# RWKV recurrence with 120 instructions of scheduler priority in a hybrid trunk layer

## The chip, the cores and the metric

The kernel runs on one core of one Trainium2 chip. The metric is the device time of one execution in microseconds (us); of several runs the median is shown. The engines are TensorE (PE in the rows, with PEld for its weight loads), VectorE (DVE), ScalarE (ACT), GpSimd (POOL) and SyncE (SP), which issues most of the DMA. Each engine has a queue of its own and works through it in order.

## The reference

One layer of a trunk with three token mixers side by side, for 512 tokens of width 1024, in float32:

```python
h = rms_norm(x)
u, q, k, v, r_k_v_and_low_rank, gates = split(h @ w_in)
y0 = s5(u)                       # complex diagonal SSM, 32 groups x 16 channels, 64 states, then GLU
y1 = diff_attention(q, k, v)     # 4 heads, two softmaxes each
y2 = rwkv7(r, w, k, v, a, b)     # 8 heads of 64, one state matrix per head
x = x + (sum_i sigmoid(gate_i) * (y_i @ w_branch_i)) @ w_out
x = x + swiglu(rms_norm(x))
```

What the change touches is the third mixer. Its state is a 64x64 matrix per head that every token updates:

```python
sa = state @ a_t
state = state * w_t + outer(sa, b_t) + outer(v_t, k_t)
y_t = state @ r_t
```

## The kernel before

**Layout.** Activations are held transposed: the 1024 channels lie on 8 tiles of 128 partitions, the 512 tokens are the free dimension. A float32 operand is split into a high and a low part, and a product is three matmuls: high times high (L1301), low times high (L1302), high times low (L1303); the attention's value projection has the same three with the operands swapped (L1285 to L1287). Each 128x512 block of weights is loaded into the ring `wr`, cast to its high part `wh` on ACT (L1229), and its low part `wl` is subtracted out on DVE (L1230). These dense projections are the bulk of TensorE's work and run through the whole kernel.

**The recurrence.** The 8 heads of RWKV are taken in 4 pairs, two heads side by side on 128 partitions, and the 512 tokens in 8 chunks of 64. What a chunk needs of itself is prepared in parallel for all chunks (`local`, `inverse`, `join`). What is left is serial: `chain(p)` of `Rwkv`, L599 to L655, walks through the 8 chunks of a pair and hands the state Z from one to the next. One step is a ring of eight links on three engines:

- PE L623: the state meets the chunk; DVE L625, twice (one per head): the result leaves PSUM and `uv` is added to it. In the first chunk there is no state yet, and two copies on DVE (L619, L620) stand in their place;
- PE L630: the inverse of the chunk is applied; ACT L631: its copy out of PSUM;
- PE L635: the update of the state; DVE L650, twice: the new state Z, for the next L623;
- off the ring: PE L638 and L640 (the output y), ACT L642 (its copies), ACT L654 (the state times its decay).

Between these links the queues hold work of other parts: dense matmuls, the S5 mixer (`cmul`, L710 to L715 on DVE, and L943 to L947 on POOL, and the matmuls L1005 and L1009), attention (L1087 to L1199), the casts of weights.

**After the recurrence** `finish(p)` normalizes the pair's output: an inverse square root on eight numbers per partition (`rsqrt`, a shift and three Newton steps of L243, L244 and L246 on DVE), its copy to 512 columns (DVE L267), its transposition to all heads (PE L269, four of 128 columns), and DVE L671, L673 and L676, which take it out of PSUM and apply it.

**What sets the order.** The Python text issues the parts as a string says, where a letter is a part and its digits the pair or quarter (C is `chain`, F `finish`, Q a quarter of S5, X, K and A attention, G gates, I and J the inverse and the join):

```python
ORDER = ("L R00 G1 R01 R02 P0 T0 I0 R10 R12 S R11 U0 P1 R20 R22 R21 T1 H0 G1 J0 U1 I1 J1 C0 P2 T2 F0 U3 U2 Q0 C1 G3 Q1 G2 H1 I2 Q2 R31 "
         "F1 R32 R30 P3 T3 J2 G1 I3 J3 C3 G1 Q3 X0 K0 A0 G2 Y0 C2 Y1 Y2 Y3 F3 X1 K1 G1 A1 F2 X2 K2 O0 O2 O3 G2 A2 X3 K3 G3 O1 A3")
```

A scheduler of the framework then simulates the engines and puts the instructions into their queues. An instruction's priority is its place in the program; of those that are ready in its simulation, the one with the smallest goes first. So the parts are interleaved, and a part issued later fills what an earlier one leaves free. PSUM has eight banks: two for the dense products, three for RWKV, three for the rest.

In the trace pair 0 runs its chain from 157 to 191 us, pair 1 from 218 to 257, pair 3 from 346 to 373, and pair 2 from 373 to 408.

Of the kernel before, what the change touches and what calls it, by code (L numbers as in the profile page):

```python
# [34 lines left out]
NSPLIT = (6, 3, 2, 3)  # L35
ORDER = ("L R00 G1 R01 R02 P0 T0 I0 R10 R12 S R11 U0 P1 R20 R22 R21 T1 H0 G1 J0 U1 I1 J1 C0 P2 T2 F0 U3 U2 Q0 C1 G3 Q1 G2 H1 I2 Q2 R31 "
         "F1 R32 R30 P3 T3 J2 G1 I3 J3 C3 G1 Q3 X0 K0 A0 G2 Y0 C2 Y1 Y2 Y3 F3 X1 K1 G1 A1 F2 X2 K2 O0 O2 O3 G2 A2 X3 K3 G3 O1 A3")
DECAY_C = 0.5 * math.exp(-0.5)

PCOLS = {}  # L40
# [232 lines left out]
class Rwkv:  # L273
# [90 lines left out]
    def _prep(self, p):  # L364
# [20 lines left out]
        cum3 = cum.rearrange("p (c t) -> p c t", t=CH)  # L385
        nc.scalar.activation(W[:, :, 1:CH + 1], cum3, AF.Exp, scale=-DECAY_C)
        wc = E.small("wc", [P, NCH], bufs=5)
        nc.gpsimd.tensor_copy(wc, W[:, :, CH])
        IW = E.slot("IW")
        nc.scalar.activation(IW, cum, AF.Exp, scale=DECAY_C)  # L390
        E.free(cum)
# [1161 lines left out]
def trunk_kernel(ctx: ExitStack, tc: tile.TileContext, A, outT):  # L1553
# [46 lines left out]
    rw = Rwkv(E, (A["w_lora"], A["g2"]))  # L1600
# [31 lines left out]
    prs, qs, qkv = [None] * 4, [None] * 4, [None] * 4  # L1632
# [4 lines left out]
            E.free(rw.xw, rw.xa)  # L1637

    def chain(p):
        rw.chain(prs[p])  # L1640

    def finish(p):
        rw.finish(p, prs[p], ydr[2][p])
# [19 lines left out]
    def glu(i):  # L1663
        gh, gl = br[0]
        dense(A["w_glu"][i], 4, lambda k: gh[:, k], lambda k: gl[:, k], lambda ps: s5.finish(i, ps, ydr[0][i]))

    step = dict(T=lambda p: rw.local(prs[p]), L=lora, R=rw_in, P=prep, I=lambda p: rw.inverse(prs[p]), J=lambda p: rw.join(prs[p]), C=chain, S=s5.params, H=s5.phases, U=s5_in, Q=s5.quarter,
                F=finish, X=att_q, K=att_kv, A=att, G=gate, Y=gelu, O=glu)
    for t in ORDER.split():
# [179 lines left out]
```

## Time and profile before

| | |
|---|---|
| three runs, us | 1003.09, 1004.07, 1008.0 (median 1004.07) |
| the profiled execution | 1011.66 us, of which its span is 1009.9 us |
| granted clock of TensorE, mean | 0.988 |
| PE busy | 970.1 us (96% of the span) |
| PEld busy | 824.2 us (82%) |
| DVE busy | 754.3 us (75%) |
| ACT busy | 473.5 us (47%) |
| POOL busy | 143.3 us (14%) |
| the chain of work that ended last | PE 77%, DVE 15%, DMA 3% |

A row of the timeline has the start and the length in us, the engine, the line of the kernel, the operation, what it writes and reads, the shapes, and in brackets the idle time of its engine ahead of it and what ended that. A row of the windows has a stretch, its length, each engine's busy time and number of instructions, the granted clock of TensorE (1.00 is 2.4 GHz, 0.50 is 1.2 GHz), the busy share of the DMA engines and GB/s.

### The profile page before, as it was taken

The numbers are of one execution on the slowest core, as the hardware profiler recorded it, in microseconds if no ns is written. First come the engines' busy times: TensorE is split into PE (matmuls) and PEld (weight loads), VectorE is DVE, ScalarE is ACT, GpSimd is POOL, SyncE is SP. The second block draws the span as 40 slices with busy tenths as digits, with TensorE's granted clock in tenths as the row PEclk, the third lists the DMA queues.
The fourth block names the chain that finished last, engine by engine and source line by source line (L and its number), as shares of the span: only waits on it lengthen the run. The fifth ranks groups of instructions, "written<-read, shape, count | busy, mean of one in ns | idle before, by whom it ended". The sixth has DMA issues, their size and how long they took to land.

```text
span 1009.9 us, 17883 instructions
## 1 busy us (share of the span) xinstructions
PE 970.1 (96%) x6416; PEld 824.2 (82%) x6416; DVE 754.3 (75%) x1941; ACT 473.5 (47%) x978; POOL 143.3 (14%) x176
## 2 busy tenths in 40 slices
PE   7989999899999999999999999989999999999998
PEld 5777777676779777888887788879999999988886
DVE  6899676789994789977867655679989998943331
ACT  6534333434342566446446324566666666632220
POOL 2021120422420001000000332011211221000000
PEclk9999899999998999999999999999999999999999
DMA  7325242221431334252448864476776677354440
GB/s 241 116 53 133 64 110 78 84 56 53 100 96 40 95 105 116 84 156 75 154 149 270 273 194 159 138 178 165 151 163 175 152 153 170 79 155 123 131 136 27
DMA packets 105593, 129.95 MB, mean 129 GB/s; under 512 B 45376, under 2 KB 47296, under 8 KB 105504
## 3 DMA queue, kind: packets, MB, share of 16 engines
q1 hardware_dynamic: 99168, 117.28, 38.7%
q0 software_dynamic: 6336, 11.54, 7.4%
q8 instruction: 50, 0.82, 0.3%
q14 instruction: 39, 0.32, 0.1%
HBM read 109.90 MB, written 18.88 MB: 128 GB/s over the span
## 4 chain that ended last, share of the span: by engine, by line
PE 77%; DVE 15%; DMA 3%; ACT 2%; issue 2%; POOL 1%; SPq 0%; DVEq 0%; ACTq 0%; POOLq 0%
PE bank L1391 21%; PE bank L1302 13%; PE bank L1303 13%; PE bank L1301 13%; DVE wl L1230 2%; DMA ar<-in_w_ffn_in 1%; DMA ar<-ymix 1%; PE bank L468 1%; PE bank L479 1%; PE bank L1188 1%; PE bank L262 1%; PE bank L630 1%; PE bank L1285 1%; PE bank L1286 1%; PE bank L1287 1%
## 5 line engine op out<-in xcount | busy, mean ns | idle before, releaser
L1229 ACT CAST wh<-wr 128x512 fp32r<-128x512 f32 x198 | 120.4, 611 | 208.8 <-PE bank L1302 163.6
L1230 DVE TENSOR_TENSOR wl<-wr,wh 128x512 fp32r<-128x512 f32 x198 | 136.8, 693 | 82.8 <-ACT wh L1229 82.3
L1301 PE MATMUL bank<-act_hi,wh 128*128 128x512 f32 x360 | 150.5, 418 | 7.8 <-ACT wh L1229 5.9
L1302 PE MATMUL bank<-act_lo,wh 128*128 128x512 f32 x360 | 149.7, 416 | 0.8 <-DVE act_lo L257 0.7
L1303 PE MATMUL bank<-act_hi,wl 128*128 128x512 f32 x360 | 149.6, 416 | 0.0
L1391 PE MATMUL bank<-sp_t,wh 128*128 128x256 f32 x528 | 97.5, 285 | 1.1 <-ACT ar L1423 0.8
L1391 PE MATMUL bank<-act_hi,wh 128*128 128x256 f32 x352 | 98.0, 278 | 0.0
L1391 PE MATMUL bank<-act_hi,wl 128*128 128x256 f32 x352 | 97.7, 278 | 0.1
L1391 PE MATMUL bank<-act_lo,wh 128*128 128x256 f32 x352 | 97.5, 277 | 0.0
L1301 PEld LDWEIGHTS bank<-act_hi,wh 128*128 128x128 f32 x360 | 70.0, 195 | 22.7 <-ACT wh L1229 5.9
L1391 PEld LDWEIGHTS bank<-sp_t,wh 128*128 128x128 f32 x528 | 82.7, 193 | 1.5 <-ACT ar L1423 1.0
L1302 PEld LDWEIGHTS bank<-act_lo,wh 128*128 128x128 f32 x360 | 70.0, 194 | 16.4 <-DVE act_lo L257 3.5
L1303 PEld LDWEIGHTS bank<-act_hi,wl 128*128 128x128 f32 x360 | 70.0, 194 | 14.4 <-issue 0.6
L1391 PE MATMUL bank<-sp_t,wl 128*128 128x256 f32 x264 | 75.2, 285 | 0.0
L1301 PE MATMUL bank<-act,wh 128*128 128x512 f32 x176 | 68.5, 389 | 0.0
L1302 PE MATMUL bank<-act,wh 128*128 128x512 f32 x176 | 68.5, 389 | 0.0
L1303 PE MATMUL bank<-act,wl 128*128 128x512 f32 x176 | 68.5, 389 | 0.0
L1391 PEld LDWEIGHTS bank<-act_hi,wl 128*128 128x128 f32 x352 | 66.2, 188 | 0.7 <-DVE wl L254 0.7
L1391 PEld LDWEIGHTS bank<-act_hi,wh 128*128 128x128 f32 x352 | 66.4, 189 | 0.3
L1391 PEld LDWEIGHTS bank<-act_lo,wh 128*128 128x128 f32 x352 | 66.4, 189 | 0.0
L253 ACT CAST wh<-ar 128x512 fp32r<-128x512 f32 x79 | 48.2, 622 | 28.1 <-DMA ar<-in_w_ffn_in 18.1
L254 DVE TENSOR_TENSOR wl<-ar,wh 128x512 fp32r<-128x512 f32 x79 | 53.1, 685 | 9.4 <-ACT wh L253 8.9
(491 smaller groups left out, 2217.7 us busy)
## 6 DMA issues: line engine op xcount, KB each, us to landing
wr<-in_w_in SPq DMA_DIRECT2D x88, 256.0 KB, 2.9
ar<-in_w_ffn_in SPq DMA_DIRECT2D x46, 256.0 KB, 3.2
wr<-in_w_ffn_out SPq DMA_DIRECT2D x40, 256.0 KB, 2.7
gate<-ar SPq DMA_DIRECT2D x24, 256.0 KB, 2.4
wr<-in_w_branch SPq DMA_DIRECT2D x24, 256.0 KB, 3.6
ar<-gate SPq DMA_DIRECT2D x24, 256.0 KB, 3.6
ar<-in_w_ffn_in POOLq DMA_DIRECT2D x22, 256.0 KB, 3.9
sp_raw<-in_w_ffn_in SPq DMA_DIRECT2D x21, 256.0 KB, 3.4
```

Of the source, the lines that this page charges most:

```text
L253: nc.scalar.copy(hi, src)
L254: nc.vector.tensor_tensor(lo, src, hi.bitcast(F32), ALU.subtract)
L262: self.nc.tensor.matmul(ps[:, b, :], sq[:, b * P:(b + 1) * P], self.c("sel"), start=True, stop=True)
L468: nc.tensor.matmul(pa[:, c * P:(c + 1) * P], kb[rows, 4 * q + c].rearrange("p a t -> p (a t)"), ar[rows, 4 * q + c].rearrange("p a t -> p ...
L479: nc.tensor.matmul(pt[64:128, w], aam[q][0:64, c, h, 1], uv[0:64, 4 * q + c, h * CH:(h + 1) * CH], start=True, stop=True)
L630: nc.tensor.matmul(pu[:, 0:P], yt[:, c0:c0 + 2].rearrange("p c t -> p (c t)"), ts, start=True, stop=True)
L1229: nc.scalar.copy(wh, raw)
L1230: nc.vector.tensor_tensor(wl, raw, wh.bitcast(F32), ALU.subtract)
L1301: nc.tensor.matmul(ps, wh[:, j], hi(k), start=k == 0, stop=False)
L1302: nc.tensor.matmul(ps, wh[:, j], lo(k), start=False, stop=False)
L1303: nc.tensor.matmul(ps, wl[:, j], hi(k), start=False, stop=k == nk - 1)
L1391: nc.tensor.matmul(ps, w[x][:, c], b(y, j), start=first and j == js[0] and n == 0, stop=last and j == js[-1] and n == 2, skip_group_check= ...
```

## The change

Everything that `chain` issues gets a priority 120 places ahead of its own. The computation, the tiles and the set of instructions on every engine stay as they are; only the order of the queues differs. Lines after the new constant are one higher, those after `chain(p)` three higher.

```diff
+CHAIN_AHEAD = 120
 DECAY_C = 0.5 * math.exp(-0.5)
...
     def chain(p):
-        rw.chain(prs[p])
+
+        with tc.high_priority(offset=CHAIN_AHEAD):
+            rw.chain(prs[p])
```

The queues of PE, DVE and ACT differ from about 155 us of the trace on and are the same again after about 445 us. In that stretch the chain's matmuls stand 5 places earlier on PE on average (from 7 later to 16 earlier), its DVE instructions 3 and its ACT instructions one. On POOL and on SP a few instructions change places with a neighbour.

The first place is on DVE, in the seventh chunk of pair 0. L619 and L620 are already the first copies of pair 1's chain; `s_rr`, `s_ri` and the `ar` tiles of L710 to L714 are S5's. Before:

```order
L650 SCALAR_TENSOR_TENSOR rw_Z_220<-bank_86,wc_rw_472,Zw_rw_1487 64x64 x2
L711 TENSOR_TENSOR ar_14_82<-s_ri_806,ar_14_82 128x512
L625 TENSOR_TENSOR rw_T_223<-bank_85,ar_2_70 64x64 x2
L712 TENSOR_TENSOR ar_12_80<-ar_12_80,ar_14_82 128x512
L619 COPY rw_T_223<-ar_5_73 64x64
L620 COPY rw_T_223<-ar_5_73 64x64
L714 TENSOR_TENSOR ar_14_82<-s_ri_806,ar_14_82 128x512
L650 SCALAR_TENSOR_TENSOR rw_Z_221<-bank_87,wc_rw_472,Zw_rw_1501 64x64 x2
```

And now (a line number is one higher, so L651 is L650 of before):

```order
L651 SCALAR_TENSOR_TENSOR rw_Z_220<-bank_86,wc_rw_472,Zw_rw_1487 64x64 x2
L711 TENSOR_TENSOR ar_12_80<-s_rr_805,ar_14_82 128x512
L626 TENSOR_TENSOR rw_T_223<-bank_85,ar_2_70 64x64 x2
L712 TENSOR_TENSOR ar_14_82<-s_ri_806,ar_14_82 128x512
L620 COPY rw_T_223<-ar_5_73 64x64
L621 COPY rw_T_223<-ar_5_73 64x64
L713 TENSOR_TENSOR ar_12_80<-ar_12_80,ar_14_82 128x512
L651 SCALAR_TENSOR_TENSOR rw_Z_221<-bank_87,wc_rw_472,Zw_rw_1501 64x64 x2
L715 TENSOR_TENSOR ar_14_82<-s_ri_806,ar_14_82 128x512
```

The chain's instructions have moved up by one S5 product each: L714 of before now stands behind the second L650, and four other instructions still stand between L625 and L650.

The second place is on DVE, at the end of `finish(0)` and the first chunk of pair 1. `rqt_rw`, `rqy_rw` and `ri_rw` are the Newton steps of that `finish`, the small `ar` tiles those of S5. Before:

```order
L710 TENSOR_TENSOR ar_6_74<-s_rr_805,ar_14_82 128x512
L246 SCALAR_TENSOR_TENSOR ri_rw_480<-rqt_rw_487,rqy_rw_494 128x8
L711 TENSOR_TENSOR ar_13_81<-ar_12_80 128x8x2
L713 TENSOR_TENSOR ar_12_80<-ar_12_80 128x8x2
L267 COPY ar_8_76<-ri_rw_480 128x512
L712 TENSOR_TENSOR ar_12_80<-ar_12_80,ar_13_81 128x8x2
L714 TENSOR_TENSOR ar_13_81<-ar_12_80 128x8x2
L711 TENSOR_TENSOR ar_12_80<-s_ri_806,ar_14_82 128x512
L715 TENSOR_TENSOR ar_12_80<-ar_12_80,ar_13_81 128x8x2
L710 TENSOR_TENSOR ar_12_80<-ar_12_80 128x8x4
L671 TENSOR_TENSOR ar_7_75<-ar_7_75,bank_86 128x512
```

And now, from the same S5 product on:

```order
L711 TENSOR_TENSOR ar_6_74<-s_rr_805,ar_14_82 128x512
L244 TENSOR_TENSOR rqt_rw_487<-rqy_rw_494 128x8
L712 TENSOR_TENSOR ar_13_81<-ar_12_80 128x8x2
L714 TENSOR_TENSOR ar_12_80<-ar_12_80 128x8x2
L245 TENSOR_TENSOR rqt_rw_487<-rqt_rw_487,rqx_rw_481 128x8
L713 TENSOR_TENSOR ar_12_80<-ar_12_80,ar_13_81 128x8x2
L715 TENSOR_TENSOR ar_13_81<-ar_12_80 128x8x2
L247 SCALAR_TENSOR_TENSOR ri_rw_480<-rqt_rw_487,rqy_rw_494 128x8
L711 TENSOR_TENSOR ar_12_80<-ar_12_80 128x8x4
L716 TENSOR_TENSOR ar_12_80<-ar_12_80,ar_13_81 128x8x2
L268 COPY ar_8_76<-ri_rw_480 128x512
```

L267 (now L268) has moved behind four small instructions of S5 that stood behind it: L712, L714, L710 and L715. The last L243 and L244 of the Newton steps have moved behind the S5 product L710 that opens both pieces. Behind L268 nine small instructions follow, and then L672 (L671 of before). On PE one dense matmul that stood ahead of the four L269 now stands behind them; between them and L635 there are five, as before.

The third place is on DVE at about 410 us, where `finish(2)` and attention run. `wl_116` is the low part of a weight block of the value projection. Before:

```order
L243 TENSOR_TENSOR rqt_rw_487<-rqi_rw_483 128x8
L244 TENSOR_TENSOR rqt_rw_487<-rqt_rw_487,rqx_rw_481 128x8
L1230 TENSOR_TENSOR wl_116<-wr_114,wh_115 128x512
L246 SCALAR_TENSOR_TENSOR rqy_rw_490<-rqt_rw_487,rqi_rw_483 128x8
L243 TENSOR_TENSOR rqt_rw_487<-rqy_rw_490 128x8
```

And now:

```order
L1164 TENSOR_REDUCE mx_s_3362<-bank_89 128x1
L677 SCALAR_TENSOR_TENSOR ar_7_75<-ar_8_76,pcol,bank_86 128x512
L1163 TENSOR_TENSOR bank_90<-bank_90,const 128x128
L247 SCALAR_TENSOR_TENSOR rqy_rw_972<-rqt_rw_969,rqi_rw_965 128x8
L1097 TENSOR_TENSOR ar_11_79<-bank_83,ar_11_79 64x512
L1164 TENSOR_REDUCE mx_s_3362<-bank_90 128x1
L244 TENSOR_TENSOR rqt_rw_969<-rqy_rw_972 128x8
L1231 TENSOR_TENSOR wl_116<-wr_114,wh_115 128x512
L1169 TENSOR_TENSOR nb_s_3371<-mx_s_3362,nrq_s_3759 128x2
```

The low part of that block now stands behind 30 instructions more, down to L1096 (now L1097), while the first matmul that reads it (L1287) stands where it stood, but for one place.

## Rows read from the trace of the kernel before

**Rows 1.** The page's span, and busy time of each engine.
```profile
span 1009.9 us, 17883 instructions
...
PE 970.1 (96%) x6416; PEld 824.2 (82%) x6416; DVE 754.3 (75%) x1941; ACT 473.5 (47%) x978; POOL 143.3 (14%) x176
```

**Rows 2.** Windows of 50 us in the stretch that the change reorders.
```profile
200.00:250.00 50.00, 46.33 (x352) 35.72 (x351) 45.40 (x129) 18.49 (x45) 13.83 (x18) 1.00 0.21 56
...
400.00:450.00 50.00, 48.60 (x294) 40.30 (x293) 42.90 (x139) 26.03 (x61) 1.27 (x1) 1.00 0.39 119
```

**Rows 3.** Waits of PE: us in total, times, the longest.
```profile
PE bank L623 <- DVE rw_Z L650: 5.4, 3, 3.3
PE bank L269 <- DVE ar L267: 3.1, 3, 1.4
...
PE bank L635 <- DVE ar L671: 1.8, 1, 1.8
...
PE bank L630 <- DVE rw_T L625: 0.8, 3, 0.4
...
PE bank L1183 <- DVE ar L1179: 0.6, 1, 0.6
```

**Rows 4.** Timeline of DVE from 179.4 to 186.4 us, seventh chunk of pair 0.
```profile
179.47 0.89 DVE L711 TENSOR_TENSOR ar<-s_ri,ar 128x512 f32<-128x512 f32 x1
...
180.89 0.98 DVE L712 TENSOR_TENSOR ar<-ar,ar 128x512 f32<-128x512 f32 x1
181.90 1.16 DVE L619 COPY rw_T<-ar 64x64 f32<-64x64 f32 x1
183.09 1.14 DVE L620 COPY rw_T<-ar 64x64 f32<-64x64 f32 x1
184.26 1.52 DVE L714 TENSOR_TENSOR ar<-s_ri,ar 128x512 f32<-128x512 f32 x1
185.82 0.58 DVE L650 SCALAR_TENSOR_TENSOR rw_Z<-bank,wc_rw,Zw_rw 64x64 f32<-64x64 f32 x2
```

**Rows 5.** Timeline of POOL in the same stretch.
```profile
181.40 1.61 POOL L945 TENSOR_TENSOR ar<-ar 128x512 f32<-128x512 f32 x1
183.09 1.10 POOL L947 TENSOR_TENSOR ar<-s_pi,ar 128x512 f32<-128x512 f32 x1
```

**Rows 6.** Windows: behind the wait at 186 us, and around `finish(0)`.
```profile
187.00:190.40 3.40, 3.40 (x13) 2.84 (x11) 2.75 (x7) 1.58 (x3) 1.12 (x2) 0.50 0.42 109
...
222.50:229.10 6.60, 3.35 (x17) 2.21 (x16) 6.60 (x12) 1.21 (x2) 6.44 (x5) 1.00 0.30 84
```

**Rows 7.** Timeline of DVE from 223.9 to 228.2 us, `finish(0)` among S5.
```profile
223.96 1.07 DVE L713 TENSOR_TENSOR ar<-ar 128x16 f32<-128x16 f32 x1
224.95 0.41 DVE L267 COPY ar<-ri_rw 128x512 f32<-128x512 f32 x1
225.29 1.25 DVE L712 TENSOR_TENSOR ar<-ar,ar 128x16 f32<-128x16 f32 x1
226.46 0.17 DVE L714 TENSOR_TENSOR ar<-ar 128x16 f32<-128x16 f32 x1
...
227.15 1.07 DVE L715 TENSOR_TENSOR ar<-ar,ar 128x16 f32<-128x16 f32 x1
```

**Rows 8.** Timeline of POOL, first and last of five S5 products there.
```profile
222.29 1.63 POOL L943 TENSOR_TENSOR ar<-s_pr,ar 128x512 f32<-128x512 f32 x1 [11.31 <-DMA gate<-ar]
...
228.15 1.14 POOL L946 TENSOR_TENSOR ar<-s_pr,ar 128x512 f32<-128x512 f32 x1
```

**Rows 9.** Timeline of PE, dense matmuls behind L635, five apart.
```profile
229.59 0.40 PE L1301 MATMUL bank<-act_hi,wh 128*128 128x512 f32 x1
...
230.76 0.39 PE L1303 MATMUL bank<-act_hi,wl 128*128 128x512 f32 x1
```

**Rows 10.** Window from the end of L1230 for `wl_116` to the end of L1096.
```profile
410.45:419.46 9.01, 8.95 (x59) 7.81 (x59) 8.71 (x29) 5.01 (x10) 0.00 (x0) 1.00 0.17 58
```

**Rows 11.** Timeline of PE: the first matmul that reads `wl_116`.
```profile
417.31 0.28 PE L1287 MATMUL bank<-wl,act_hi 128*128 128x256 f32 x1
```

## The prediction

> **What bounds the kernel now.** I read the page's shares first: PE is busy 970.1 of 1009.9 us [rows 1]. So the kernel is a full TensorE queue with some 40 us of holes, and a new order can win only holes, or make new ones. The reader should next see how far the other engine of the chain has room: DVE is busy 45.40 of 50 us in the window from 200 us and 42.90 in the one from 400 us [rows 2]. An instruction that is moved up in such a queue puts something else back, and what is put back may be wanted too.
>
> Then the waits of PE [rows 3]. Three kinds belong to the recurrence: L623 for the new state (5.4 us in three waits, one of them 3.3), L630 for its operand (0.8), and L635 for a PSUM bank that L671 of `finish` holds (1.8). That is 8.0 us, all that the change aims at, 0.8% of the span. The same view shows that `finish` is as much in the way: L269 waits for L267 three times, 3.1 us in all.
>
> The timeline of the longest wait tells what it is made of [rows 4]. After L625 the DVE queue holds L712, L619, L620 and L714 (0.98 + 1.16 + 1.14 + 1.52 = 4.80 us), and only then L650, for which PE waits. Beside it stands POOL's timeline [rows 5]: L945 ends at 181.40 + 1.61 = 183.01 and the copy L619 at 181.90 + 1.16 = 183.06; L947 ends at 184.19 and the copy L620 at 184.23. Two 64x64 copies of over 1.1 us, each ending 0.04 to 0.05 us after a POOL product: DVE stands still until POOL is done. The Trainium skill gives the reason ("SBUF — State Buffer", section "Who interferes with whom"): the two engines share a pair of ports, the one that holds it keeps it for its whole instruction, and the other blocks. By that rule, with which the trace agrees, an instruction that is moved up one place only meets the next POOL product; were the ports shared by the cycle, term 1 would be at its lower end.
>
> **The change part by part.** No instruction is added or removed, so every term is a wait that shrinks, grows or is new. The profiled execution took 1011.66 us (span 1009.9), 7.6 us or 0.76% above the median of the three runs, 1004.07; the sum is made against the profiled one and its difference is applied to the median. A measurement of this kernel can tell about 0.5%, 5 us, from no change.
>
> *Term 1, the wait of 3.3 us (first place in the order).* L714 moves behind L650, but another S5 product, L711, comes from ahead of L625 to behind it, and the copies of pair 1's chain, which have the same priority, stay in between. Four instructions as before. If each kept the length of its row [rows 4], the queue would shrink by 1.52 - 0.89 = 0.63 us, which is the most. If each waits for a POOL product as the copies do, their number is the same and only an earlier start is left. PE itself arrives earlier too, since one matmul fewer stands between L623 and L630. I take -0.2 us, near the reading that the copies' rows show, between -0.6 and +0.5 (two matmuls of cover lost).
>
> *Term 2, `finish(0)` (second place).* Its L267 moves behind L712, L714, L710 and L715. The first and the last took 1.25 and 1.07 us [rows 7], beside five POOL products that run from 222.29 to 229.29 [rows 8]; L714 took 0.17, and L710 is of its size. That is 2.7 us. L269 starts 2.7 us later, and as one dense matmul (0.23 us, from five steps in 230.76 - 229.59 = 1.17 [rows 9]) now stands behind it, its wait grows by 2.9, from 1.4 to 4.3. Behind L267 the queue to L671 becomes shorter: those four are gone from there (2.7), and nine small ones come (1.5 at 0.17). A 512-wide product leaves as well; I set it against the later of the nine being wider. With the same five matmuls of cover on PE the wait of L635 shrinks by 1.2, from 1.8 to 0.6. Together +2.9 - 1.2 = +1.7 us. Below: the four meet no POOL product and cost 0.17 each, 0.7 in all; 0.7 + 0.2 - 1.2 = -0.3. Above: three more POOL products at 1.1 are waited for, and L635 gains nothing: +3.5. I take +1.7, since the rows show every S5 product there held that reads two tiles while POOL works.
>
> *Term 3, the weight block at 410 us (third place).* The low part `wl_116` is ready at 410.45, where the window [rows 10] begins, 6.9 us before its first use at 417.31 [rows 11]. That distance is its cover. It now stands behind everything down to L1096: 29 instructions, with 8.71 us of DVE in 9.01 [rows 10], so DVE has no slack there to catch up. It is ready at 410.45 + 8.71 = 419.16, and PE waits 1.85 us. The wait of L1183 for L1179 (0.6) [rows 3] comes 5 us later, is DVE's too, and is then covered. +1.2 us, between 0 (pair 2's chain has released DVE two microseconds sooner) and +2.5 (nothing is given back, and the few small ones that come in addition count).
>
> *The rest of the chains.* Pair 2 has the most other work between its links: on PE 137 other instructions before and 127 now, on DVE 76 and 70. Ten matmuls of 128 to 512 columns are 1.2 to 2.3 us of cover that PE no longer has when it reaches a link; six DVE instructions at 42.90/139 = 0.31 [rows 2] are 1.9 us of queue that the link no longer stands behind. They cancel. Pairs 1 and 3 lose three or four matmuls each. I take 0, between -1.5 and +1.5. POOL and SP swap neighbours only; no transfer is among PE's waits in this stretch, so that costs nothing, and if one came late it would show as a wait of L1301 for L1229.
>
> The sum is -0.2 + 1.7 + 1.2 + 0 = **+2.7 us**: 1014.4 for a profile like this one, and 1004.07 + 2.7 = **1006.8 us** for the median. With the terms' lower ends it would be -2.4 (1001.7); upper ends together lead into the second rival.
>
> **The rivals.** *The waits of the chain go.* If DVE serves each link at once, 8.0 us go. Behind the longest wait PE also ran at half its clock: granted 0.50, which is 1.2 GHz, for 3.4 us [rows 6], work that takes 1.7 us at 2.4 GHz. Together 9.7 us: 994.4 us. For it speaks that the links wait for DVE alone and that this is what the change raises. Against it: in the longest wait, 3.3 of the 5.4 us at L623, four instructions still stand ahead of L650. It counts as faster from 5 us on.
>
> *The put-back work becomes the bound (the other side).* The mechanism is that of term 2, at the same place: L267 behind three more POOL products. With its upper end (+3.5), term 3's (+2.5), and +0.5 in term 1, 6.5 us are lost. A wait of over 4 us at L269 is longer than the 3.3 that left PE at half clock, so 1.7 us for such a stretch [rows 6] may come on top: +8.2, 1012.3 us. It decides from about 5 us, that is when term 2 is above its middle and the clock falls. For it: DVE is busy for the whole 6.60 us of that window. Against it: in the same window PE sat idle for 6.60 - 3.35 = 3.25 us, in several pieces, and its clock stayed at 1.00 [rows 6]. The Trainium skill ("TensorE: Matmul & The Clock Gate", section "HAM oscillation — how this bites in real kernels") warns that a loop's waits send the clock back to its low rate each time they come; the row from 187 us agrees, and the one from 222.5 us doesn't.
>
> *It cancels to nothing.* The scheduler moves links by five places on PE, with four still in front on DVE; late work that I see as waited for is early enough after all. 1004.1 us.
>
> **How the numbers follow.** The forecast gets 0.42, the change that cancels 0.10, the waits that go 0.13, the put-back work 0.35: I have followed two places by hand where something is put back and none where a long wait really ends, but each upper end needs several things at once. The forecast and the cancelling lie within 0.5% (999.0 to 1009.1): 0.52. Faster 0.13, slower 0.35. The range that should hold the time 8 times in 10 goes down to 999.0, where it leaves out the waits that go, and up to 1012.5, just above the second rival; the forecast's own range is 1001.7 to 1009.
>
> **What would show it.** Term 1: the wait of PE at L623 (now L624) in pair 0's chain stays between 2.6 and 3.5 us with L619 and L620 still over 1.1. Term 2: a wait at L269 of about 4 us and the one at L635 under 1; if L267 follows L246 without two instructions of over 1 us between, it is wrong. Term 3: a wait of L1287 for L1230, which the list of before doesn't have. The clock: a window at 0.50 behind L269, or none. The forecast is wrong if L623's waits together fall under 2 us without such new ones, or if PE's waits for `finish` and for the casts grow by over 5.

## The result and the profile after

The changed kernel takes 1010.71 us (median of 9 runs, 1008.98 to 1016.86); the kernel before takes 1005.9 beside it (9 runs, 1003.09 to 1008.72). The ratio is 1.0057, interval [1.0033, 1.0081]: slower by a little more than the 0.5% that I had called measurable. Forecast was +2.7 us, and the medians lie 4.8 us apart. The profiled execution took 1016.86 us, the slowest of the nine. (The ratios are worked out over the single runs without disturbed ones, so they need not be the quotient of two medians.)

The page of after, span and busy time (to be held against [rows 1]):

```profile
span 1015.1 us, 17874 instructions
...
PE 977.2 (96%) x6416; PEld 829.5 (82%) x6416; DVE 752.6 (74%) x1941; ACT 472.7 (47%) x978; POOL 136.7 (13%) x176
...
PE 77%; DVE 13%; DMA 4%; ACT 3%; issue 2%; POOL 1%; SPq 0%; DVEq 0%; ACTq 0%; POOLq 0%
```

No instruction is new, yet PE is busy 7.1 us longer (977.2 against 970.1). The same matmuls can take longer only where they run slower, so the granted clock is the next thing to look at. The waits of PE after (us in total, times, the longest; compare [rows 3]):

```profile
PE bank L270 <- DVE ar L268: 4.4, 2, 3.5
PE bank L624 <- DVE rw_Z L651: 2.5, 2, 2.2
...
PE bank L1288 <- DVE wl L1231: 0.9, 1, 0.9
PE bank L639 <- ACT ar L632: 0.7, 1, 0.7
...
PE bank L631 <- DVE rw_T L626: 0.4, 1, 0.4
...
PE bank L636 <- ACT ar L632: 0.4, 1, 0.4
```

The chain's waits did shrink: L624 (L623 of before) from 5.4 to 2.5 us, L631 (L630) from 0.8 to 0.4. The bank of L636 (L635) is no longer waited for on account of `finish`. In exchange L270 (L269) went from 3.1 to 4.4, and one single wait of it is now 3.5. A wait of 0.9 at L263 for L677 of `finish`, at 282 us, is new too:

```profile
PE bank L263 <- DVE ar L677: 0.9, 1, 0.9
```

All holes of PE over 0.3 us between 150 and 450 us add up to 12.2 us before and 10.4 after. So by its holes alone the change gains 1.8 us in the stretch that it reorders; the loss is not an idle PE.

The timeline of DVE after, at the first place (compare [rows 4]):

```profile
183.84 1.00 DVE L712 TENSOR_TENSOR ar<-s_ri,ar 128x512 f32<-128x512 f32 x1
184.88 0.98 DVE L620 COPY rw_T<-ar 64x64 f32<-64x64 f32 x1
185.90 0.19 DVE L621 COPY rw_T<-ar 64x64 f32<-64x64 f32 x1
186.12 1.64 DVE L713 TENSOR_TENSOR ar<-ar,ar 128x512 f32<-128x512 f32 x1
187.79 0.58 DVE L651 SCALAR_TENSOR_TENSOR rw_Z<-bank,wc_rw,Zw_rw 64x64 f32<-64x64 f32 x2
```

Four instructions as forecast, but one of the two copies met no POOL product and took 0.19 us. At the second place, first DVE, then POOL (compare [rows 7, 8]):

```profile
225.64 1.08 DVE L244 TENSOR_TENSOR rqt_rw<-rqy_rw 128x8 f32<-128x8 f32 x1
226.64 0.17 DVE L712 TENSOR_TENSOR ar<-ar 128x16 f32<-128x16 f32 x1
226.73 1.08 DVE L714 TENSOR_TENSOR ar<-ar 128x16 f32<-128x16 f32 x1
...
227.90 1.25 DVE L715 TENSOR_TENSOR ar<-ar 128x16 f32<-128x16 f32 x1
229.07 0.15 DVE L247 SCALAR_TENSOR_TENSOR ri_rw<-rqt_rw,rqy_rw 128x8 f32<-128x8 f32 x1
229.15 0.18 DVE L711 TENSOR_TENSOR ar<-ar 128x32 f32<-128x32 f32 x1
229.25 1.07 DVE L716 TENSOR_TENSOR ar<-ar,ar 128x16 f32<-128x16 f32 x1
230.25 0.41 DVE L268 COPY ar<-ri_rw 128x512 f32<-128x512 f32 x1
```

```profile
225.02 1.67 POOL L944 TENSOR_TENSOR ar<-s_pr,ar 128x512 f32<-128x512 f32 x1 [12.26 <-DVE ar L711]
226.65 1.12 POOL L945 TENSOR_TENSOR ar<-s_pi,ar 128x512 f32<-128x512 f32 x1
227.86 1.26 POOL L946 TENSOR_TENSOR ar<-ar,ar 128x512 f32<-128x512 f32 x1
229.20 1.10 POOL L948 TENSOR_TENSOR ar<-s_pi,ar 128x512 f32<-128x512 f32 x1
```

Each POOL product stands beside one DVE instruction of a few columns that ends with it: 226.69 and 226.72, 227.77 and 227.81, 229.12 and 229.15, 230.30 and 230.32. Before, the copy L267 started 2.66 us after the first POOL product of this group (224.95 - 222.29) and had sat out two of them; now L268 starts 5.23 us after it (230.25 - 225.02) and has sat out four. PE pays at this line:

```profile
230.72 1.11 PE L270 MATMUL bank<-ident,ar 128*128 128x128 f32 x4 [3.53 <-DVE ar L268]
```

And what followed is in the windows of after, around that wait and behind it (compare the clock of 1.00 in [rows 6]):

```profile
225.00:230.00 5.00, 2.19 (x11) 1.48 (x10) 5.00 (x12) 1.21 (x2) 4.83 (x4) 0.95 0.36 112
229.50:236.30 6.80, 5.58 (x16) 4.64 (x17) 6.27 (x22) 0.40 (x1) 2.12 (x2) 0.50 0.01 4
```

PE worked 2.19 of 5.00 us. From 229.5 to 236.3 us the clock stood at 0.50, that is 1.2 GHz; PE worked 5.58 us of that, so some 2.8 us are lost. In the order of before the same place stayed at 1.00, with its idle time in two pieces of 1.42 and 1.82 us.

For every run its span and its mean granted clock are known, so that span x (1 - clock) is the time that it lost to the half clock, a little too much where PE was idle in such a stretch. For the two profiled executions that is 1015.1 x 0.019 = 19.3 us after and 1009.9 x 0.012 = 12.1 before: the 7 us by which PE is busy longer. Only the 2.8 us are made at this wait. The largest other piece that before does not have lies ahead of everything that the change reorders, and 3.4 us are lost in it:

```profile
134.00:140.80 6.80, 6.80 (x45) 5.10 (x46) 3.05 (x11) 1.34 (x3) 0.00 (x0) 0.50 0.14 41
```

### The profile page after: what moved, and what is told of

Its sections match the earlier page's. It is cut to its first block, busy times and chain, and to the rows that moved or that the text cites. A ratio compares the mean times of both kernels' runs of the same rounds, so it can differ in the third digit from the quotient of the medians.

```text
span 1015.1 us, 17874 instructions
## 1 busy us (share of the span) xinstructions
PE 977.2 (96%) x6416; PEld 829.5 (82%) x6416; DVE 752.6 (74%) x1941; ACT 472.7 (47%) x978; POOL 136.7 (13%) x176
## 4 chain that ended last, share of the span: by engine, by line
PE 77%; DVE 13%; DMA 4%; ACT 3%; issue 2%; POOL 1%; SPq 0%; DVEq 0%; ACTq 0%; POOLq 0%
PE bank L1392 21%; PE bank L1303 13%; PE bank L1304 13%; PE bank L1302 13%; DVE wl L1231 2%; DMA ar<-in_w_ffn_in 1%; PE bank L469 1%; DMA ar<-ymix 1%; PE bank L1288 1%; PE bank L1286 1%; PE bank L1287 1%; PE bank L480 1%; PE bank L263 1%; PE bank L636 1%; PE bank L1189 1%
## 5 line engine op out<-in xcount | busy, mean ns | idle before, releaser
L1230 ACT CAST wh<-wr 128x512 fp32r<-128x512 f32 x198 | 120.3, 611 | 209.8 <-PE bank L1303 159.6
L1231 DVE TENSOR_TENSOR wl<-wr,wh 128x512 fp32r<-128x512 f32 x198 | 138.2, 700 | 85.5 <-ACT wh L1230 84.9
L1303 PE MATMUL bank<-act_lo,wh 128*128 128x512 f32 x360 | 152.8, 424 | 0.8 <-DVE act_lo L258 0.7
L1304 PE MATMUL bank<-act_hi,wl 128*128 128x512 f32 x360 | 152.3, 423 | 0.0
L1304 PEld LDWEIGHTS bank<-act_hi,wl 128*128 128x128 f32 x360 | 71.5, 199 | 13.9 <-issue 0.4
```

Of the source, the lines that this page charges most:

```text
L1230: nc.scalar.copy(wh, raw)
L1231: nc.vector.tensor_tensor(wl, raw, wh.bitcast(F32), ALU.subtract)
L1303: nc.tensor.matmul(ps, wh[:, j], lo(k), start=False, stop=False)
L1304: nc.tensor.matmul(ps, wl[:, j], hi(k), start=False, stop=k == nk - 1)
```

## The experiments

Theory A, formed from this comparison: the loss is made in `finish(0)`. The copy that was put back makes one long wait, and behind it PE drops to half clock; what the chain gains elsewhere is smaller. The rivals stand in the expectations. The scheduler makes the queues anew for every kernel, so an edit of the work changes the order in other places as well.

**Which pair's priority does it.** Three kernels give the priority to some of the pairs alone. This is the edit for pair 0; the others have `(1, 2, 3)` and `(2,)` in its place:

```diff
     def chain(p):
-        rw.chain(prs[p])
+        if p in (0,):
+            with tc.high_priority(offset=CHAIN_AHEAD):
+                rw.chain(prs[p])
+        else:
+            rw.chain(prs[p])
```

Pair 0 alone:

> Priority for pair 0's chain alone. Its DVE queue has the first and the second place of the prediction as the changed kernel has them (four instructions in front of the second L650; L267 of finish(0) behind four small S5 instructions), and the low part wl_116 only 4 places later instead of 26. Theory A (the loss sits at finish(0), where L267 waits behind POOL): most of the loss of the changed kernel, +3 to +5 us, with a wait of about 3.5 us at L269 near 230 us and half clock behind it. Theory B (the loss is spread over the four chains): about a quarter, +1 to +1.5 us. Theory C (the loss is only half-clock stretches that come and go by chance): no difference from before in the median, 0 +- 2 us, with runs of equal granted clock equal in time.

Pairs 1, 2 and 3:

> Priority for the chains of pairs 1, 2 and 3, not for pair 0. The first and second place are as before the change; wl_116 stands 15 places later. Theory A: within 1.5 us of before, with the wait of 3.3 us at L623 and those of 1.4 and 1.8 us at L269 and L635 as before. Theory B: three quarters of the loss, +3 to +4 us. Theory C: 0 +- 2 us.

Pair 2 alone:

> Priority for pair 2's chain alone (372 to 408 us). wl_116 stands 15 places later than before, instead of 26. If the third place matters by itself, a wait of L1287 for L1230 of up to 1 us is there and the wait of L623 near 392 us (1.15) goes: 0 to +1 us. Theory A: within 1 us of before. Theory B: +1 to +1.5 us. Theory C: 0 +- 2 us.

Measured against one set of 35 runs of the kernel before (median 1009.91): pair 0 alone 1011.21 us, ratio 1.0022 [0.9998, 1.0046]; pairs 1 to 3 1011.51, 1.0032 [1.0011, 1.0053]; pair 2 alone 1012.35, 0.9996 [0.997, 1.0022]. PE's first matmul of `finish(0)` in the three profiles, in that order:

```profile
225.44 0.65 PE L270 MATMUL bank<-ident,ar 128*128 128x128 f32 x4 [3.52 <-DVE ar L268]
```

```profile
224.93 0.66 PE L270 MATMUL bank<-ident,ar 128*128 128x128 f32 x4 [1.42 <-DVE ar L268]
```

```profile
221.39 0.66 PE L270 MATMUL bank<-ident,ar 128*128 128x128 f32 x4 [1.42 <-DVE ar L268]
...
225.03 0.46 PE L636 MATMUL bank<-ar 128*128 128x128 f32 x2 [1.83 <-DVE ar L672]
```

So the wait of 3.5 us comes with pair 0's priority, and without it it doesn't come. The times that theory A gave missed: +3 to +5 us for pair 0, where the medians lie 1.3 apart, and less than 1.5 for pairs 1 to 3, where they lie 1.6 apart. The ratios do not sort the three, and the reason is instructive: the second and the third of these kernels turned out to have the same instructions in the same order on all five engines. Beside pair 2's, the priority of pairs 1 and 3 changes no queue at all; the whole change is that of pairs 0 and 2. One program, measured twice on one chip, gave 1.0032 and 0.9996. What a single ratio of this kernel can tell is therefore hardly better than 0.4%. With the half clock of each run taken off, pair 0 alone stands at 999.8 us (standard error 0.8), the kernel before at 999.7 (0.3), and the two sets of runs of the other program at 1000.6 (0.3): what there is of a loss beyond the clock is with pair 2's part, and it is about twice its error.

These kernels correct a reading of mine too. At the first place their order is that of before, and the wait there is 2.3 us in both of them (the waits of PE with the priority for pairs 1 to 3):

```profile
PE bank L624 <- DVE rw_Z L651: 4.5, 3, 2.3
PE bank L270 <- DVE ar L268: 3.1, 3, 1.4
...
PE bank L636 <- DVE ar L672: 1.8, 1, 1.8
```

The 3.3 us of [rows 3] are one of two outcomes of the same order. The second copy and a POOL product start together. In the profile of before both start at 183.09 and the copy takes 1.14 us [rows 4, 5]; here, DVE and then POOL, both start at 183.54 and the copy takes 0.19:

```profile
183.54 0.19 DVE L621 COPY rw_T<-ar 64x64 f32<-64x64 f32 x1
```

```profile
183.54 1.16 POOL L948 TENSOR_TENSOR ar<-s_pi,ar 128x512 f32<-128x512 f32 x1
```

The long outcome is that of the profile of before and of one more below (3.29, the copy written five times), the short one that of these two and of the kernel with S5's steps on POOL (2.30). So the change's 2.2 is less by 1.1 or by 0.1.

**The change once more**, with the clock of each run:

> The change as it is, beside the runs of before on the chip of these experiments, with the granted clock of every run on both sides. Theory A (the loss sits at finish(0): a wait of 3.5 us at L269 and half clock behind it): +3 to +6 us; the wait is there again within 0.2 us, since the order sets it; with each run's half-clock time taken off (its span times one minus its clock), the two kernels differ by less than 1.5 us. Theory C (only half-clock stretches that come and go by chance): within 2 us of before, and the same mean clock.

Measured: 1011.39 us (12 runs) against 1007.64 (19), ratio 1.0036 [1.0018, 1.0055]. The wait at L270 is 3.52 us again, and behind it the clock is low again:

```profile
223.64 0.66 PE L270 MATMUL bank<-ident,ar 128*128 128x128 f32 x4 [3.52 <-DVE ar L268]
...
226.23 0.76 PE L636 MATMUL bank<-ar 128*128 128x128 f32 x2 [0.35 <-DVE ar L713]
```

```profile
224.50:228.50 4.00, 3.65 (x12) 2.54 (x11) 3.79 (x17) 0.18 (x1) 0.05 (x1) 0.57 0.00 0
```

The clock was at 0.50 for 3.4 us, PE worked 3.05 of them, and some 1.5 us are lost here. Over the runs, the kernel before lost 8.9 us a run at half clock and the change 11.0: +2.1 us (standard error 0.9). The rest of the time went from 998.95 (standard error 0.44) to 1000.62 (0.55): +1.7, where theory A allowed less than 1.5. The clock is thus about half of the loss. The other part is not to be seen in the stretch that the change reorders. Its queues differ up to 496 us, not 445 as I wrote, and from 150 to 500 us PE is idle for 14.5 us in this profile and for 14.6 before. Behind 500 us, where the order is the same, it is 13.6 against 11.6; but over all profiles of this document that part lies anywhere between 10.5 and 13.9, so one execution can't tell.

**The wait made by hand.** No priority, but `finish(0)` writes its copy five times:

```diff
-    def head_bc(self, ps, v):
+    def head_bc(self, ps, v, more=0):
...
-        self.nc.vector.tensor_copy(w.rearrange("p (g n) -> p g n", n=64), v.unsqueeze(2).broadcast_to([P, 8, 64]))
+        for _ in range(1 + more):
+            self.nc.vector.tensor_copy(w.rearrange("p (g n) -> p g n", n=64), v.unsqueeze(2).broadcast_to([P, 8, 64]))
...
-            E.head_bc(pb, ri)
+            E.head_bc(pb, ri, 4 if p == 0 else 0)
```

> No priority; the copy of finish(0) to 512 columns (L267) is written five times instead of once, so that L269 waits longer, and nothing else is changed by hand. It measures the disputed wait by itself. Theory A: the wait at L269 grows from 1.4 to some 5 us or more, half clock follows it, and the time grows by the added wait and about 1.7 us more: +4 to +7 us. Theory C: the added wait alone, as far as no other wait shrinks, without a change of the mean clock: +1 to +3 us.

Measured: 1016.05 us (6 runs), ratio 1.0075 [1.0048, 1.0103]; the means of the runs lie 7.7 us apart (1015.54 and 1007.85). Of these +5.0 us are half clock (13.9 lost a run against 8.9) and +2.7 the rest. The wait and the window behind it:

```profile
227.12 1.11 PE L271 MATMUL bank<-ident,ar 128*128 128x128 f32 x4 [4.36 <-DVE ar L269]
```

```profile
225.40:232.20 6.80, 5.08 (x15) 4.31 (x16) 5.92 (x21) 1.33 (x3) 0.30 (x1) 0.50 0.07 25
```

A hole of this kind at this place, with no priority anywhere, brings the half clock behind it, and the kernel is clearly slower. That much of theory A stands. How much of the 7.7 us (+4 to +7 were expected) this hole costs is not shown: half clock behind it costs some 2.5 us here, the wait of 1.8 us at L635 has gone, and from this place on the queues differ from those of before, with another wait of 2.67 us at L271 at 278 us.

**The copy of `finish` on ACT** (no priority; the question is whether the copy itself is what comes late):

```diff
-        self.nc.vector.tensor_copy(w.rearrange("p (g n) -> p g n", n=64), v.unsqueeze(2).broadcast_to([P, 8, 64]))
+        self.nc.scalar.copy(w.rearrange("p (g n) -> p g n", n=64), v.unsqueeze(2).broadcast_to([P, 8, 64]))
```

> No priority; the copy to 512 columns (L267), in all its uses, is on ACT instead of DVE. The waits of L269 in finish (3.1 us in three) lose DVE's queue but keep the Newton steps in front: -0.5 to -2 us if L267's own place in DVE's queue matters, no change if the Newton steps are what is late.

Measured: 1008.43 us, ratio 1.001 [0.9982, 1.0037]. No gain, and the wait grew from 1.42 to 2.78 us:

```profile
221.15 0.66 PE L270 MATMUL bank<-ident,ar 128*128 128x128 f32 x4 [2.78 <-ACT ar L268]
```

The Newton steps ahead of the copy are still on DVE, and their last, L247, now stands behind L714 and L715, which took 1.08 and 1.25 us beside POOL, as in the changed kernel. The copy alone was not what comes late.

**The two copies of the chain on ACT** (no priority; a test of term 1):

```diff
-                    nc.vector.tensor_copy(ts[B, B], uv[R, c, B])
-                    nc.vector.tensor_copy(ts[R, R], uv[R, c, R])
+                    nc.scalar.copy(ts[B, B], uv[R, c, B])
+                    nc.scalar.copy(ts[R, R], uv[R, c, R])
```

> No priority; the two copies that stand for the first link of every chain (L619, L620) are on ACT instead of DVE. The two of pair 1 lie in front of L650 in the longest wait of before and cost DVE 2.3 us there, since each waits for a POOL product. If that reading is right, the wait of 3.3 us at L623 falls by 1 us or more, and the half clock of 187 to 190 us may go with it: -1 to -4 us. If the wait has another cause, it stays near 3.3 us and the time is that of before.

Measured: 1011.85 us, ratio 1.0032 [1.0002, 1.0063]. The wait at the first place fell to 1.22 us, as that reading says, but another of 1.18 at L631 came next to it and one of 1.81 at L263 later. The time is a miss (-1 to -4 us were expected): the wait that was taken away came back in other places.

**S5's doubling steps on POOL** (no priority), meant to free DVE around `finish(0)`:

```diff
-        E, V = self.E, self.E.nc.vector
+        E, V = self.E, (self.E.nc.gpsimd if hf else self.E.nc.vector)
```

> No priority; the doubling of S5's phases (second half: the small L710 to L715 that stand among the Newton steps of finish(0)) runs on POOL instead of DVE. L267 then stands right behind the 512-wide S5 product. If it is the small instructions that meet POOL which hold L267, the waits of L269 (1.4) and L635 (1.8) near 225 us go: -1 to -3 us. If POOL's queue becomes the bound (36 more instructions there), waits for L943 to L947 appear and the time grows.

Measured: 1015.94 us, ratio 1.0085 [1.0055, 1.0115]. The waits of `finish(0)` at L269 and L635 did go, so it is small S5 instructions that held its copy. The time is a miss all the same: POOL's own queue became the bound. PE waits, then DVE:

```profile
235.35 0.80 PE L624 MATMUL bank<-rw_Z,ar 128*128 128x128 f32 x2 [9.85 <-DVE rw_Z L651]
```

```profile
233.50 1.19 DVE L949 SCALAR_TENSOR_TENSOR ar<-ar,ar 128x512 f32<-128x512 f32 x1 [9.41 <-POOL ar L947]
```

```profile
227.00:240.50 13.50, 5.15 (x26) 4.25 (x27) 4.97 (x15) 1.89 (x5) 9.59 (x19) 0.51 0.12 40
```

**An offset of 40** instead of 120 (`CHAIN_AHEAD = 40`, all pairs):

> The change with 40 instead of 120. On DVE the first place is as in the changed kernel, and at the second L267 stands behind the last S5 step and two of the next instead of behind four, wl_116 9 places later instead of 26. Theory A: the wait at L269 lies between the 1.4 of before and the 3.5 of the changed kernel, and the time between the two: 0 to +3 us. Theory B (the loss grows with what the chains put back): also between. Theory C: 0 +- 2 us.

Measured: 1015.44 us (8 runs), ratio 1.0068 [1.0039, 1.0097]. That is above the 1.0036 of 120, though the intervals overlap, and above everything that was expected (0 to +3 us; the medians lie 7.8 apart). It has a wait of 3.19 us at L270 at 225 us and one of 2.91 at 273, each followed by a stretch at half clock; 14.7 us a run are lost at the clock, and the rest is 1.0 above that of before. The offset is not a dial: a third of it gives another order with its own holes.

**No POOL product to wait for.** The five products of S5 at L943 to L947 go from POOL to DVE, first without priority, then with that of the change:

```diff
-        G.tensor_tensor(F[0], a_r, c_r, ALU.mult)
+        V.tensor_tensor(F[0], a_r, c_r, ALU.mult)
...
-        G.tensor_tensor(t0, a_i, c_r, ALU.mult)
+        V.tensor_tensor(t0, a_i, c_r, ALU.mult)
```

Without priority:

> No priority; S5's five products per quarter that ran on POOL (L943 to L947) run on DVE. POOL then reads nothing beside DVE in these places. If a POOL product is what holds the copies and the small instructions, L619 and L620 of pair 1 take about 0.2 us instead of 1.1, the longest wait at L623 near 185 us falls below 1.5 us, and L246, L713, L712 and L715 of 222 to 228 us take 0.2 each; the price is 5 x 0.7 = 3.5 us more on DVE in each of four quarters. Time: -3 to +1 us. If the cause lies elsewhere they stay over 1 us and the time grows by up to 5 us.

The same again:

> The kernel without priority and with S5's five products on DVE once more, since its first interval reached just past no change. If the gain is real: -2 to -5 us, with the longest wait at L623 of pair 0 below 1 us, L269 of finish(0) without a wait over 0.3 us, and the span less its half-clock time some 4 us under that of before. If the first one was luck: 0 +- 2 us.

With the change's priority:

> The change, with those five products on DVE. If theory A is right (the change costs what it does through the wait at L269, and that wait is made of instructions that POOL holds), the wait of 3.5 us falls to 2 us or less although L267 stands behind 19 small instructions, now at 0.1 to 0.2 us each, and the time is within 2 us of the kernel without priority and with the products on DVE. If it is the order by itself that costs, it stays 3 us or more above that one.

Without priority: 1004.36 us against 1007.16, ratio 0.9981 [0.9955, 1.0008], and 1008.02 against 1008.48, 0.9996 [0.997, 1.0022]. The copies at the first place are short now (DVE's timeline in the second profile):

```profile
183.22 0.19 DVE L620 COPY rw_T<-ar 64x64 f32<-64x64 f32 x1
183.42 0.19 DVE L621 COPY rw_T<-ar 64x64 f32<-64x64 f32 x1
```

1.16 and 1.14 us beside POOL [rows 4], 0.19 without it. The wait behind them is gone, too. By the lock of the Trainium skill's "SBUF — State Buffer", section "Who interferes with whom", this is what must happen, and these rows agree. Time less that lost at half clock falls by 4.3 and 3.8 us (994.1 against 998.4, 995.4 against 999.2). But the loss at half clock rises by nearly as much, from 8.5 to 11.5 and from 9.2 to 12.9, and nothing is left that could be measured. Both profiles show the same new stretch of half clock, this one in the second:

```profile
153.00:165.00 12.00, 12.00 (x89) 9.00 (x89) 3.71 (x12) 2.67 (x8) 0.52 (x1) 0.50 0.07 23
```

Ahead of it PE is not idle: from 120 us on its timeline has no hole of 0.3 us. Why the clock falls there stays open; the last section says what PE ran just before.

With the priority: 1011.07 us, ratio 1.0035 [1.0007, 1.0062] against before, and above the same kernel without it by 6.8 us in the medians and 5.4 in the means. No wait of L270 for L268 is over 0.25 us. So theory A is only half the truth: with its wait taken away, the order of the change still costs something. Of the 5.4 us half clock is 3.1 (14.6 a run against 11.5), and 2.4 are the rest. The chain's own waits are longer here (L631 3.0 us in seven, the longest 1.0, against 0.9 in four; L624 1.4 against 0.6), which fits links that reach PE with less other work ahead of them. But other waits are shorter: from 150 to 500 us PE is idle for 10.4 us with the priority and for 10.4 and 9.7 in the two profiles without. So the 2.4 us are not located either.

## Why the prediction was right, and where its size was off

The direction and the place were right. The forecast was +2.7 us; the medians lie 4.8 and 3.75 us apart in two sets of runs. The 1010.7 us stand above the forecast's own range (1001.7 to 1009) and inside the wide one. Of the 3.9 us between them and the forecast of 1006.8, 1.8 come from the kernel before, whose nine runs have a median of 1005.9 where the first three had 1004.07. By the 5 us from which I let the put-back work decide, the result is on the border of that rival, which had 0.35.

*Term 1* (-0.2): right in sign, though I held it against a number that is only one of two. The wait is 2.2 us where I said 2.6 to 3.5. The order of before has 3.3 or 2.3, as the second copy loses or wins against POOL; the change is worth -1.1 or -0.1. One of the copies was held by POOL (0.98), the other wasn't (0.19), so "two copies over 1.1" was wrong: how the queues stand against each other differs from order to order.

*Term 2* (+1.7): the mechanism holds. L268 starts 2.57 us later behind its POOL products (5.23 against 2.66; forecast 2.7), and the wait is 3.53 (forecast 4.3; 2.9 was taken as its growth and 2.1 measured, since PE itself came to L269 0.5 us later behind the first POOL product: 2.17 us against 1.71). By my own test for it, two instructions of over 1 us between L247 and L268, only one stands there (L716, 1.07); the other, L715 (1.25), is just ahead of L247, and the Newton step L244 is held too (1.08). The sum of what is held is the same. The wait of L635 went wholly (1.82 to 0, or 0.35 in the second profile; forecast 0.6). As holes that is 3.53 to 3.87 us instead of 3.24: only +0.3 to +0.6.

*The step that failed* is the one that left the clock out of this place. I put the half clock into the second rival and had it decide "from about 5 us", at a wait of over 4 us. One piece of 3.5 us was enough, and the 4.3 us that the forecast itself gave the wait were over that mark, so its sum should have had the 1.7 us. Across the profiles, the first wait at L269, that at L635, and how long the clock stood at 0.50 at their end (half of it is lost as far as PE works: 1.5 us where it begins in the wait or has a hole, 1.7 where not, 2.5 and 2.8 in the two long ones):

| kernel | wait at L269 | at L635 | at 0.50 |
|---|---|---|---|
| before | 1.42 | 1.82 | 0 |
| priority for pairs 1 to 3 | 1.42 | 1.81 | 3.4 |
| priority for pair 2 (same program) | 1.42 | 1.83 | 0 |
| chain's copies on ACT | 1.23 | 2.01 | 0 |
| `finish`'s copy on ACT | 2.78 | 1.41 | 0 |
| offset 40 | 3.19 | none | 3.4 |
| pair 0 alone | 3.52 | none | 3.4 |
| the change, second profile | 3.52 | 0.35 | 3.4 |
| the change, first profile | 3.53 | none | 6.8 |
| copy written five times | 4.36 | none | 6.8 |

About the same idle time in two pieces left the clock alone in four of five executions; in one piece, or nearly in one, it cost the clock in five of five. The length of a hole does not settle it alone: the changed kernel's wait of 2.19 us at the first place was followed by 3.4 us at 0.50 in its first profile, and by none in its second. The forecast moved idle time from two holes into one and priced it by its sum alone. With 1.7 us for it the whole sum would have been +4.4. The Trainium skill's "TensorE: Matmul & The Clock Gate", section "HAM oscillation — how this bites in real kernels", tells of a long wait that brings back the low rate; the table agrees with it.

*Term 3* (+1.2): the wait is there but shorter, 0.87 us of L1288 for L1231 (forecast 1.85), and that of L1183 for DVE (0.6) has gone. Both together +0.3 us. Where the other microsecond went I have not followed.

*The rest of the chains* (0, between -1.5 and +1.5): the waits of 0.98 and 1.15 us at L623 in the chains of pairs 3 and 2 went, and 0.73, 0.40 and 0.44 us at L639, L636 and L631 came: -0.6.

Summed up, holes: -0.1 + 0.3 + 0.3 - 0.6 = -0.1 us, where I had +2.7 without the clock. No term of mine had the others: 0.92 at L263 came, and 0.91 at L269, 0.38 at L630 and 0.38 at L1188 went, which is some -0.7. (With -1.1 for term 1 that is the fall of 1.8 us between the first two profiles.) The measured +3.75 of the second set of runs consists of 2.1 us of clock (uncertain by 0.9) and 1.7 us that are not located (uncertain by 0.7, from the standard errors). I was nearer to the time than my terms deserve.

*The rivals.* That the chain's waits go: about half of them went (L623 and L630 from 6.2 us, or 5.2 with the short outcome at the first place, to 2.9), and the time did not follow. The put-back work: it came, at its place, by its mechanism, at a smaller price (half of 8.2 us) and with the clock falling earlier than I said.

What stays open: the 1.7 us beyond clock and holes; why the order alone still costs with no POOL product in the way; and what makes the clock fall at 152 us with PE busy.

## What to carry to other kernels

A higher priority for one serial chain is a reordering of every queue: read which instruction is put back, who waits for it, and on which other engine's work it will have to sit there. Price a hole by its length and by what the clock does behind it: two short ones and a long one of the same sum were not the same here. Before believing half a per cent, look at the granted clock of each run, and measure one program twice.

## What was unexpected

The time at half clock varies from run to run in an unchanged program: 35 runs of the kernel before on one chip took 1001.5 to 1015.8 us, and lost between 2.0 and 16.2 us at half clock, by span x (1 - clock). Even ahead of 150 us, where the queues are the same, the first profiles differ: the mean granted clock was 0.97 before and 0.94 after.

The clock also fell without a hole: in both profiles of the kernel with S5's products on DVE a stretch of some 14 us from about 153 us on ran at 0.50, with PE busy throughout, and where the kernel before ran at 1.00. An edit that shortens the work by 4 us was paid back by it. Nor is that peculiar to this kernel. The profile of before has such a stretch at 310 us, with no hole of 0.3 us since 292:

```profile
309.90:316.70 6.80, 6.80 (x53) 5.93 (x54) 2.46 (x10) 1.30 (x3) 0.00 (x0) 0.50 0.10 39
```

In both kernels PE had just finished the 32 small matmuls, 32x32 each, that end `join` (L584 of before, here L585 in the kernel with S5's products on DVE):

```profile
152.30 0.74 PE L585 MATMUL bank<-ar,ar 32*32 32x32 f32 x30
```

They also stand just ahead of the stretch at 134 us in the profile of after. Elsewhere the clock stayed at 1.00 behind them (at 157 us in the profile of before), and no run here tests whether they are the reason.
